# An encoder layer with expert retrieval on one core: row gathers without a pacing copy, value pieces fetched one at a time, the two halves of a weight made apart, and four accumulator banks filled ahead of the last group

## The chip, the cores and the metric

The kernel runs on one core of a Trainium2 chip. The metric is the device time of one execution in microseconds (us). Three timed runs of the kernel before gave 3643.04, 3645.47 and 3650.47 us; the median, 3645.47 us, is what the changed kernel is compared with. One further execution was recorded by the hardware profiler; all rows below come from it.

## The reference, cut to what matters

The layer has an attention half and a retrieval half (PEER). The change touches only the retrieval half, which takes 512 tokens of width 2048 and, per token, 8 heads with 16 experts each out of 16384:

```python
def block(args):
    xt, et, gt = args                                   # tokens, expert numbers, gates
    a = jnp.einsum('td,thkd->thk', xt, u_tab[et])
    w = gt * jax.nn.gelu(a, approximate=False)
    return jnp.einsum('thk,thkd->td', w, v_tab[et])
...
x = layer_norm(DN_ALPHA * x + g2 * p, ln2_g[l], ln2_b[l])
```

## The kernel before, in words

**Two ways to the same sum.** For the first 352 tokens (TD) the kernel computes every expert densely: u times tokens for all 16384 experts, gelu, times a gate that is zero where an expert was not chosen, times v. For the other 160 tokens it gathers only the chosen rows of u and v, one expert row per token and instruction: 320 gathers of 128 rows of 8 KB (1 MB each), 160 of u and then 160 of v. The dense part is the work of TensorE, the gathered part that of VectorE (DVE), which multiplies a gathered row by the token and sums (L1058), or adds a row, scaled, to an accumulator (L1064).

**Precision.** Each fp32 matmul is done as three in a reduced format: a tensor is split in a high part (a copy on ScalarE, ACT) and a low part (a subtraction on DVE), and hi*hi, hi*lo and lo*hi are summed. So each piece of weights needs a DMA (`raw`), a copy on ACT (`whi`, L99) and a subtraction on DVE (`wlo`, L100) before TensorE can use it.

**The stream.** The class Stream (L49) hands out pieces of 128x1024 (512 KB) in the order of a plan. `get` takes the next piece and then calls `fill`, which emits the split of the piece three places ahead (`split` is 3) and the loads up to six ahead (`ahead` is 6, L876). There are five buffers each for raw, high and low parts, so piece i takes over the buffers of piece i-5. Within the plan an expert row block of u has two pieces (`u`, x=0 and 1), and so has a tile of v.

**Groups and tiles.** 128 blocks of 128 experts make 32 groups of four (GE). Fourteen groups (0 to 13) have their u part computed in earlier stages and stored; the other 18 are in `gorder`. The main loop (L1230) goes over these 18: for each of four j it computes the u block (`u_mm`, 48 matmuls of 352 columns), the gelu (ACT, L1235), and then `v_mm` (L1166) for tile j of the group before. `v_mm` makes four units dd of 12 matmuls; a unit has its own PSUM bank, one of six, and needs all four weights W of a group (`W_0` to `W_3`, each high and low). Both v pieces are taken at its start (L1170): the first serves the W with x=0 and 1, the second those with x=2 and 3. After each unit ACT copies the bank to `accT` (L1185; L1187 in group 12) and fills the bank of the unit four later with the sum so far (`copy_in`, L1163). Between the units the functions of the list `beside` are emitted, one after each unit: the product of gelu and gate (`gl`, DVE, L1143), then `pair`, the high part (ACT, L1146) and the low part (DVE, L1147) of the next group's W. A short loop (L1246) does the last v group of the 18 with no u beside it, and the final part (L1370) goes over the stored groups 0 to 13, with v alone.

**The rows.** `step` (L1217) emits the gathers that are due at a fixed rate: twice per tile in the main loop (after the gelu and after `v_mm`), once per tile in the short loop and, at 0.85 of the rate, in the final part. `gather` (L1073) takes one of three row buffers, emits the pacing copy, the indirect DMA (both on GpSimd, POOL) and the use of the row of two calls before (LAG is 2) on DVE. The pacing copy (`paced`, L292 to L296) writes one column of the row buffer out of the newest `wlo`, so that the DMA cannot start before that split is done.

**What sets the order.** In these stages `inorder` is 2, and every instruction under `pin(op, 2)` keeps its place in the program on its engine. The rest (stores, loads of `x1`, the multiplication at L94, nearly all of the last group) is placed by the tile scheduler. On POOL, in order: the row copies and row DMAs, the loads of gates (`load_g`, L1134), the loads of stored gelu (`load_0` L1227, `load_gl` L1359), which wait until the low part W has been made out of the same buffer.

**The last group.** In group 13 the output is computed with tokens on the partitions: `start_sum` (L1342) fills a bank with `x1` (ACT, L1345), adds the transposed `accT` by matmuls (L1348, L1351), and `v_part` (L1204) adds group 13. Its v pieces are first multiplied by a gate (DVE, L94).

```python
        v = [st.get("v", g, j, x) for x in range(2)]
...
                vh, vl = v[x // 2]
                wh, wl = W[g, x]
                s = slice(x % 2 * 512 + dd * P, x % 2 * 512 + (dd + 1) * P)
```

Of the kernel before, what the change touches and what calls it, by code (L numbers as in the profile page):

```python
# [15 lines left out]
AF = mybir.ActivationFunctionType  # L16
# [3 lines left out]
P = 128  # L20
# [106 lines left out]
def tile_encoder_layer(ctx: ExitStack, tc: tile.TileContext, a: dict, out: bass.AP):  # L127
# [84 lines left out]
    def pin(op, level=1):  # L212


        if inorder[0] >= level:
            tc.keep_in_program_order(op)
        return op
# [74 lines left out]
    def paced(t, src=None, eng=nc.vector):  # L292


        src = st.parts[max(st.parts)][1] if src is None else src
        return eng.tensor_copy(t[:, 0:1], src.bitcast(F32)[:, 0:1])  # L296
# [775 lines left out]
    def gather(n=1):  # L1072

        for _ in range(n):
            i = ng[0]
            if i < NROW:
                ng[0] += 1
                row = gr.tile([P, D], F32, tag="row", name=f"row{i}")
                pin(paced(row, None, nc.gpsimd), 2)
                w, n_, c = gitems[i]  # L1080
                off = bass.IndirectOffsetOnAxis(ap=tiles[n_][0][:, c : c + 1], axis=0)
                src = a["peer_u"] if w == "u" else a["peer_v"]
                pin(nc.gpsimd.indirect_dma_start(out=row, out_offset=None, in_=src, in_offset=off), 2)
                rows_in.append((gitems[i], row))
            if len(rows_in) > (LAG if i < NROW else 0):
                gather_use()
# [39 lines left out]
    for q4 in range(XQ):  # L1126
        nc.gpsimd.dma_start(h2x[q4 * XT : (q4 + 1) * XT], h2x_d)
    ww = ctx.enter_context(pool("W", 2 * GE))
    W = {}

    def load_g(wk, g, gt=None):
        if gt is None:
# [4 lines left out]
    def weigh(gl, gt, g, j):  # L1137

        hi, lo = W[g, j] = [ww.tile([P, TD], F32R, tag="W" + n, name=f"W{g}_{j}{n}") for n in "hl"]

        def product():
            v3 = gl.rearrange("p (t c) -> p t c", t=NCH)
            pin(nc.vector.tensor_tensor(out=v3, in0=v3, in1=gt[:, :, j, :], op=ALU.mult), 2)  # L1143

        def pair():
            pin(nc.scalar.activation(hi, gl, AF.Copy), 2)  # L1146
            pin(nc.vector.tensor_tensor(out=lo, in0=gl, in1=hi.bitcast(F32), op=ALU.subtract), 2)  # L1147

        return [product, pair]

    banks("peer", q=2, o=6)
    ob_ = [bank("o") for _ in range(6)]
# [6 lines left out]

    def copy_in(u):  # L1160

        if 16 <= u < nunits:
            pin(nc.scalar.activation(ob_[u % 6][:, :TD], accT[:, u % 16], AF.Copy), 2)  # L1163

    def v_mm(g, j, by=None, beside=()):

        v = [st.get("v", g, j, x) for x in range(2)]
        beside = list(beside)  # L1170
        for dd in range(4):
            u = nu[0]
            o = o_bank()[:, :TD]
            sum_ = accT[:, j * 4 + dd]
            for x in range(GE):
                vh, vl = v[x // 2]
                wh, wl = W[g, x]
                s = slice(x % 2 * 512 + dd * P, x % 2 * 512 + (dd + 1) * P)
                first, last_ = u < 16 and x == 0, x == GE - 1
                kw = dict(skip_group_check=u >= 16)  # L1180
                pin(nc.tensor.matmul(o, vh[:, s], wh, start=first, stop=False, **kw), 2)  # L1181
                pin(nc.tensor.matmul(o, vh[:, s], wl, start=False, stop=False, **kw), 2)  # L1182
                pin(nc.tensor.matmul(o, vl[:, s], wh, start=False, stop=last_, **kw), 2)  # L1183
            if by is None:
                pin(nc.scalar.activation(sum_, o, AF.Copy), 2)  # L1185
            else:
                pin(nc.scalar.activation(sum_, o, AF.Copy, scale=by[:, j * 4 + dd : j * 4 + dd + 1]), 2)  # L1187
            copy_in(u + 4)
            f = beside.pop(0) if beside else None
            if f is not None:  # L1190
                f()
        for f in beside:
            f()
# [19 lines left out]
    def step(w=1.0):  # L1213
        pace[0] += rate * w
        gather(int(pace[0]))
        pace[0] -= int(pace[0])
# [4 lines left out]
    with pool("peer", 2, "right") as wk:  # L1221
        def gl_of(g, j):
            return wk.tile([P, TD], F32, tag="gl", name=f"gl{g}_{j}", bufs=2)

        def load_0(j):
            gls[0, j] = gl_of(0, j)
            pin(nc.gpsimd.dma_start(gls[0, j], ga_d[j]), 2)  # L1227

        gls = {}
        for n, g in enumerate(gorder):  # L1230
            gt = load_g(wk, g)
            for j in range(GE):
                gl = gl_of(g, j)
                ps = u_mm(g * GE + j)
                pin(nc.scalar.activation(gl, ps[:, :TD], AF.Gelu), 2)  # L1235
                if n > 0 or j > 1:
                    step()
                work = weigh(gl, gt, g, j)
                if n > 0:
                    v_mm(gorder[n - 1], j, None, work)  # L1240
                    step()
                else:
                    for f in work:
                        f()
        gt = load_g(wk, 0)
        load_0(0)  # L1246
        load_0(1)
        for j in range(GE):
            work = [None, None] + weigh(gls[0, j], gt, 0, j)
            if j < 2:  # L1250
                work.append(lambda j=j: load_0(j + 2))
            v_mm(gorder[-1], j, None, work)
            step()


    with pool("fin", 1, "right") as wk:
# [15 lines left out]
        def cols(j, n=1):  # L1272
            return slice(j * 512, (j + n) * 512)
# [17 lines left out]
            eng.dma_start(out[t * P : (t + 1) * P, c], r[:, c])  # L1291

        last = NF // GE - 1
        x1 = {}
        stts = [wk.tile([P, 4, 6], F32, name=f"stt{t}") for t in range(NT)]
        st.by = {("v", last, j, x): g2[:, cols(j)] for j in range(4) for x in range(2)}

# [44 lines left out]
        def start_sum(t, j):  # L1342

            o = o_bank()
            nc.scalar.activation(o, x1[t][:, cols(j)], AF.Copy)  # L1345
            kw = dict(start=False, stop=False, skip_group_check=True)
            if t == ND - 1:
                nc.tensor.matmul(o, sel, accx[:, cols(j)], **kw)  # L1348
            for dd in range(4):
                ts_ = slice(t * P, t * P + rows_of(t))  # L1350
                nc.tensor.matmul(o[: rows_of(t), dd * P : (dd + 1) * P], accT[:, j * 4 + dd, ts_], ident, **kw)  # L1351
            return o
# [3 lines left out]
        def load_gl(g, j):  # L1356
            if g <= last:
                gls[g, j] = wk.tile([P, TD], F32, tag="gl", name=f"gl{g}_{j}", bufs=GE)
                pin(nc.gpsimd.dma_start(gls[g, j], ga_d[g * GE + j]), 2)  # L1359
# [5 lines left out]
        for g in range(last + 1):  # L1365


            gt1, gt = gt, load_g(wk, g + 2, gts[g % 2]) if g + 2 <= last else None
            work = []
            for j in range(GE if g < last else 0):  # L1370
                product, pair = weigh(gls[g + 1, j], gt1, g + 1, j)
                work.append([lambda j=j, g=g: parts(g, j), None, product, pair, lambda j=j, g=g: load_gl(g + 2, j)])
            if g == 0:

                wh = W[g, 0][0]
                for o in ob_:
                    nc.tensor.matmul(
                        o[:, TD:], wh[:, :P], wh[:, : S - TD], start=False, stop=True, skip_group_check=True
                    )
            if g == 2:  # L1380
                for r, n in ((l2g, "ln2_g"), (l2b, "ln2_b")):
                    nc.gpsimd.dma_start(r, a[n].to_broadcast([P, D]))
            if g == last:
                inorder[0] = 0
            for j in range(GE):
                if g < last:
                    v_mm(g, j, mod[:, 80:96] if g == last - 1 else None, work[j])
                    if g < VN:
                        step(VW)
                elif j < 2:  # L1390
                    os_ = [start_sum(t, j) for t in range(ND)]
                    v = [st.get("v", g, j, x) for x in range(2)]
                    for x in range(GE):
                        for t in range(ND):
                            v_part(os_[t], g, x, t, v[x // 2])
                    for t, o in enumerate(os_):
                        nc.vector.bn_stats(stts[t][:, j, :], o)
                        nc.scalar.activation(x1[t][:, cols(j)], o, AF.Copy)
# [20 lines left out]
def _lay(inp):  # L1419
# [21 lines left out]
    def piece(n, *k):  # L1441
# [31 lines left out]
    rel = np.clip(np.arange(P)[:, None] - np.arange(S)[None, :] + 384, -63, 256) + 63  # L1473
    u = f("peer_u")[0]
    v = f("peer_v")[0]
    freq = (np.float32(10000.0) ** (-np.arange(0, 64, 2, dtype=np.float32) / np.float32(64.0))).astype(np.float32)
    rot = np.zeros((P, 2), np.float32)
    rot[:, 0] = np.tile(freq, 4)
# [16 lines left out]
        "ln1_g": f("ln1_g"), "ln1_b": f("ln1_b"), "ln2_g": f("ln2_g"), "ln2_b": f("ln2_b"),  # L1495
        "keys_t": f("peer_keys")[0].reshape(16, P, P).transpose(2, 0, 1).reshape(P, 16 * P),
        "u_t": u.reshape(P, P, 2, 8, P).transpose(1, 2, 4, 3, 0).reshape(P, 2, P, 1024),
        "v_t": v.reshape(P, NG, 2, 2, 4, 512).transpose(1, 4, 2, 0, 3, 5).reshape(NG, 4, 2, P, 1024),
        "peer_u": u,
        "peer_v": v,  # L1500
    }
# [17 lines left out]
```

## Time and profile before

| what | value |
|---|---|
| timed runs, median (lowest to highest) | 3645.47 us (3643.04 to 3650.47) |
| the profiled execution, its own time | 3657.82 us |
| its span, first to last instruction | 3656.0 us |
| TensorE matmul busy (share of the span) | 3568.4 us (98%) |
| VectorE, ScalarE, GpSimd busy | 2695.8, 1727.1 and 1002.2 us (74%, 47%, 27%) |
| pacing copies of rows (L296, POOL) | 320, 326.4 us, 1020 ns each |
| DMA, mean over the span | 273 GB/s |

The profiled execution is 12.35 us longer than the median run. Busy times are shares of a stretch; a stage is read by the windows that cut the span, and what an engine lacked by the waits, which name for each line what ended the idle time before it. Times in rows are us from the span's start. A matmul is shown some 0.32 us long while the next starts 0.16 us after it, so a short stop of TensorE can stay hidden in its busy time; the count of matmuls in a stretch tells more.

### The profile page before, as it was taken

How to read it: one execution, taken by the hardware profiler on the slowest of the kernel's cores; microseconds unless marked ns; L12 is line 12 of the kernel's file. 1: busy time of each engine (PE TensorE's matmuls, PEld its weight loads, DVE VectorE, ACT ScalarE, POOL GpSimd, SP SyncE). 2: the span in 40 equal slices, each digit the busy share in tenths (PEclk: the TensorE clock that was granted, in tenths of full speed). 3: DMA queues.
4: the chain of work that ended last, by engine and by line, in shares of the span. 5: the costliest groups of instructions: out<-in, count | busy, mean ns of one | idle time of the engine just before them, and what ended most of it. 6: DMA issues, size and time to landing. Idle time of an engine off the chain costs nothing. (4 is left out here: it accounts for less than half of the span.)

```text
span 3656.0 us, 52881 instructions
## 1 busy us (share of the span) xinstructions
PE 3568.4 (98%) x20127; PEld 3285.5 (90%) x20127; DVE 2695.8 (74%) x3754; ACT 1727.1 (47%) x3072; POOL 1002.2 (27%) x1068
## 2 busy tenths in 40 slices
PE   8999999999999999999999999999999999899998
PEld 6888888887787889999999999999999999899997
DVE  8756587545555779988888678888777788677776
ACT  3233332233333455435666345555544455566763
POOL 0001110011120000002322344444454544455531
PEclk9999999999999999999999999999999999999999
DMA  9646488744356655446998899999989999799982
GB/s 395 259 164 227 165 303 301 261 141 130 115 193 241 203 197 159 130 132 234 339 349 329 313 355 357 351 365 360 355 327 343 331 362 368 298 345 341 346 326 93
DMA packets 216207, 996.71 MB, mean 273 GB/s; under 512 B 26817, under 2 KB 34161, under 8 KB 159345
## 3 DMA queue, kind: packets, MB, share of 16 engines
q1 hardware_dynamic: 131904, 525.93, 40.4%
q0 software_dynamic: 73104, 431.48, 31.5%
q10 hardware_dynamic: 10944, 35.94, 2.5%
q8 instruction: 157, 2.57, 0.3%
q14 instruction: 98, 0.79, 0.1%
HBM read 930.42 MB, written 61.51 MB: 271 GB/s over the span
## 5 line engine op out<-in xcount | busy, mean ns | idle before, releaser
L99 ACT ACTIVATE whi<-raw 128x1024 fp32r<-128x1024 f32 x800 | 822.7, 1055 | 773.8 <-PE main L160 491.9
L100 DVE TENSOR_TENSOR wlo<-raw,whi 128x1024 fp32r<-128x1024 f32 x800 | 959.4, 1221 | 284.1 <-ACT whi L99 280.0
L159 PE MATMUL q<-dh,whi 128*128 128x352 f32 x1680 | 546.2, 325 | 0.6 <-ACT glf L926 0.6
L161 PE MATMUL q<-dh,wlo 128*128 128x352 f32 x1680 | 542.1, 323 | 0.7 <-DVE wlo L100 0.7
L160 PE MATMUL q<-dl,whi 128*128 128x352 f32 x1680 | 542.5, 323 | 0.0
L296 POOL COPY row<-wlo 128x1 f32<-128x1 f32 x320 | 326.4, 1020 | 714.5 <-DVE wlo L100 519.7
L1064 DVE SCALAR_TENSOR_TENSOR h2g<-row,au,h2g 128x2048 f32<-128x2048 f32 x127 | 298.4, 2349 | 101.9 <-DMA row<-in_peer_v,gidx 99.3
L159 PE MATMUL main<-hh,whi 128*128 128x512 f32 x912 | 352.9, 394 | 10.1 <-ACT hh L354 9.9
L160 PE MATMUL main<-hl,whi 128*128 128x512 f32 x912 | 357.1, 392 | 0.0
L161 PE MATMUL main<-hh,wlo 128*128 128x512 f32 x912 | 349.4, 393 | 0.0
L1058 DVE SCALAR_TENSOR_TENSOR row<-row,h2g 128x2048 f32<-128x2048 f32 x128 | 292.6, 2288 | 76.8 <-DMA row<-in_peer_u,gidx 76.4
L161 PEld LDWEIGHTS q<-dh,wlo 128*128 128x128 f32 x1680 | 316.6, 188 | 1.0 <-DVE wlo L100 1.0
L159 PEld LDWEIGHTS q<-dh,whi 128*128 128x128 f32 x1680 | 316.5, 188 | 1.0 <-ACT glf L926 0.8
L160 PEld LDWEIGHTS q<-dl,whi 128*128 128x128 f32 x1680 | 317.0, 189 | 0.0
L1185 ACT ACTIVATE accT<-o 128x352 f32<-128x352 f32 x480 | 219.5, 458 | 184.2 <-PE o L1183 178.6
L300 DVE SCALAR_TENSOR_TENSOR adaw<-adaw,cond 128x2048 f32<-128x2048 f32 x96 | 218.8, 2291 | 100.7 <-DMA adaw<-in_w_ada_t 96.9
L159 PE MATMUL main<-qh,whi 128*128 128x352 f32 (+2 forms) x752 | 242.9, 323 | 7.5 <-ACT qs L950 7.4
L161 PE MATMUL main<-qh,wlo 128*128 128x352 f32 (+2 forms) x752 | 242.7, 323 | 0.0
L160 PE MATMUL main<-ql,whi 128*128 128x352 f32 (+2 forms) x752 | 242.0, 322 | 0.0
L1163 ACT ACTIVATE o<-accT 128x352 f32<-128x352 f32 x480 | 223.0, 465 | 0.0
L159 PEld LDWEIGHTS main<-hh,whi 128*128 128x128 f32 x912 | 172.1, 189 | 47.3 <-ACT hh L354 11.5
L161 PEld LDWEIGHTS main<-hh,wlo 128*128 128x128 f32 x912 | 171.7, 188 | 35.8
(1359 smaller groups left out, 8045.9 us busy)
## 6 DMA issues: line engine op xcount, KB each, us to landing
raw<-in_wst SPq DMA_DIRECT2D x288, 512.0 KB
raw<-in_u_t SPq DMA_DIRECT2D x256, 512.0 KB
raw<-in_v_t SPq DMA_DIRECT2D x256, 512.0 KB
adaw<-in_w_ada_t SPq DMA_DIRECT2D x96, 1024.0 KB
g_d<-stg ACTq DMA_DIRECT2D x11, 2048.0 KB
gt<-g_d POOLq DMA_DIRECT2D x19, 704.0 KB
ga_d<-glf ACTq DMA_DIRECT2D x56, 176.0 KB
gl<-ga_d POOLq DMA_DIRECT2D x56, 176.0 KB
```

Of the source, the lines that this page charges most:

```text
L99: self.pin(self.nc.scalar.activation(hi, raw, AF.Copy), 2)
L100: self.pin(self.nc.vector.tensor_tensor(out=lo, in0=raw, in1=hi.bitcast(F32), op=ALU.subtract))
L159: pin(nc.tensor.matmul(ps, lh, rh, start=first, stop=False), 2)
L160: pin(nc.tensor.matmul(ps, lh, rl, start=False, stop=False), 2)
L161: pin(nc.tensor.matmul(ps, ll, rh, start=False, stop=last), 2)
L296: return eng.tensor_copy(t[:, 0:1], src.bitcast(F32)[:, 0:1])
L300: pin(nc.vector.scalar_tensor_tensor(w, w, 1.0, cond, op0=ALU.mult, op1=ALU.mult, accum_out=mod[:, j : j + 1]))
L1058: op = nc.vector.scalar_tensor_tensor(row, row, 1.0, h_, op0=ALU.mult, op1=ALU.mult, accum_out=a_[:, c : c + 1])
L1064: op = nc.vector.scalar_tensor_tensor(accs[n], row, a_[:, c : c + 1], accs[n], op0=ALU.mult, op1=ALU.add)
L1163: pin(nc.scalar.activation(ob_[u % 6][:, :TD], accT[:, u % 16], AF.Copy), 2)
L1185: pin(nc.scalar.activation(sum_, o, AF.Copy), 2)
```

## The change

Four edits. `gather` no longer emits the pacing copy where `inorder` is 2; the indirect DMA is then held by its buffer and its place on POOL alone. `v_mm` takes the two v pieces one at a time, at dd 0 and dd 2, and the host lays v out so that one piece holds two output blocks dd for all four W (group 13 keeps the old layout). `pair` becomes `high` and `low`, and their places move: in the main loop product, high, then the `step` that stood after `v_mm`, then low; in the short loop step, product, high, low; in the final part product, high, low one place earlier, without the empty place. And `copy_in` also fills the banks of the first four units of group 13 with `x1`, four units ahead, in program order; `start_sum` leaves these out.

```diff
-                pin(paced(row, None, nc.gpsimd), 2)
+                if inorder[0] < 2:
+                    paced(row, None, nc.gpsimd)
...
-        def pair():
+        def high():
             pin(nc.scalar.activation(hi, gl, AF.Copy), 2)
+
+        def low():
             pin(nc.vector.tensor_tensor(out=lo, in0=gl, in1=hi.bitcast(F32), op=ALU.subtract), 2)
 
-        return [product, pair]
+        return [product, high, low]
...
-        if 16 <= u < nunits:
+        if nunits <= u < nunits + 6:
+            t, j = (u - nunits) % ND, (u - nunits) // ND
+            pin(nc.scalar.activation(ob_[u % 6], x1[t][:, j * 512 : (j + 1) * 512], AF.Copy), 2)
+        elif 16 <= u < nunits:
...
-        v = [st.get("v", g, j, x) for x in range(2)]
...
+            if dd % 2 == 0:
+                vh, vl = st.get("v", g, j, dd // 2)
             for x in range(GE):
-                vh, vl = v[x // 2]
                 wh, wl = W[g, x]
-                s = slice(x % 2 * 512 + dd * P, x % 2 * 512 + (dd + 1) * P)
+                s = slice(x * 256 + dd % 2 * P, x * 256 + (dd % 2 + 1) * P)
...
-                    v_mm(gorder[n - 1], j, None, work)
-                    step()
+                    v_mm(gorder[n - 1], j, None, work[:2] + [step, work[2]])
...
-            work = [None, None] + weigh(gls[0, j], gt, 0, j)
+            work = [step] + weigh(gls[0, j], gt, 0, j)
...
             v_mm(gorder[-1], j, None, work)
-            step()
...
             o = o_bank()
-            nc.scalar.activation(o, x1[t][:, cols(j)], AF.Copy)
+            if nu[0] > nunits + 4:
+                nc.scalar.activation(o, x1[t][:, cols(j)], AF.Copy)
...
-                product, pair = weigh(gls[g + 1, j], gt1, g + 1, j)
-                work.append([lambda j=j, g=g: parts(g, j), None, product, pair, lambda j=j, g=g: load_gl(g + 2, j)])
+                work.append([lambda j=j, g=g: parts(g, j)] + weigh(gls[g + 1, j], gt1, g + 1, j)
+                            + [lambda j=j, g=g: load_gl(g + 2, j)])
...
+    vt = v.reshape(P, NG, GE, 4, 2, 256).transpose(1, 3, 4, 0, 2, 5).reshape(NG, 4, 2, P, 1024).copy()
+    last = NF // GE - 1
+    vt[last] = v.reshape(P, NG, 2, 2, 4, 512)[:, last].transpose(3, 1, 0, 2, 4).reshape(4, 2, P, 1024)
```

## Rows read from the trace of the kernel before

**Rows 1.** Windows by stage; columns stand in the first line, idle time is not shown.
```profile
core 0: us, PE busy (x) PEld busy (x) DVE busy (x) ACT busy (x) POOL busy (x), PEclk, DMA share, GB/s
2043.00:2440.00 397.00, 395.23 (x2474) 393.24 (x2474) 319.97 (x316) 196.81 (x346) 180.59 (x160) 1.00 0.93 349
2440.00:2617.00 177.00, 177.00 (x1115) 177.00 (x1114) 145.37 (x141) 90.18 (x162) 79.94 (x75) 1.00 0.95 362
2617.00:3000.00 383.00, 371.12 (x2299) 368.45 (x2298) 296.49 (x218) 188.24 (x337) 191.94 (x151) 0.99 0.91 338
3000.00:3120.00 120.00, 120.00 (x757) 120.00 (x757) 97.56 (x75) 61.69 (x112) 53.07 (x54) 1.00 0.97 368
3120.00:3178.00 58.00, 47.50 (x239) 43.23 (x239) 34.27 (x30) 26.30 (x54) 17.29 (x22) 0.88 0.78 295
3178.00:3588.00 410.00, 396.10 (x2410) 387.80 (x2408) 314.51 (x280) 274.13 (x549) 197.54 (x176) 0.99 0.89 327
3588.00:3656.00 68.00, 55.00 (x284) 45.11 (x284) 37.23 (x52) 23.69 (x40) 10.35 (x9) 0.91 0.18 70
```

**Rows 2.** Waits from 2043 to 3588: total us, times, longest us.
```profile
POOL row L296 <- DVE wlo L100: 426.2, 124, 16.2
DVE h2g L1064 <- DMA row<-in_peer_v,gidx: 99.3, 48, 7.6
PE o L1183 <- DVE wlo L100: 21.6, 19, 3.1
PE o L1181 <- ACT W_3h L1146: 7.7, 6, 1.7
PEld o L1182 <- DVE W_3l L1147: 4.8, 13, 0.4
```

**Rows 3.** DVE's timeline in the main loop: start, length, instruction, idle before.
```profile
2706.18 2.34 DVE L1064 SCALAR_TENSOR_TENSOR h2g<-row,au,h2g 128x2048 f32<-128x2048 f32 x1
2713.11 2.35 DVE L1064 SCALAR_TENSOR_TENSOR h2g<-row,au,h2g 128x2048 f32<-128x2048 f32 x1 [4.59 <-DMA row<-in_peer_v,gidx]
2715.38 2.36 DVE L100 TENSOR_TENSOR wlo<-raw,whi 128x1024 fp32r<-128x1024 f32 x2
...
2722.19 0.52 DVE L1143 TENSOR_TENSOR gl<-gl,gt 128x352 f32<-128x352 f32 x1
```

**Rows 4.** TensorE's timeline, the matmul that stopped in the same stretch.
```profile
2716.66 0.43 PE L1183 MATMUL o<-W_2h,wlo 128*128 128x352 f32 x1 [2.13 <-DVE wlo L100]
```

**Rows 5.** POOL's timeline, the same stretch.
```profile
2700.14 4.94 POOL L296 COPY row<-wlo 128x1 f32<-128x1 f32 x1 [5.59 <-DVE wlo L100]
2705.36 0.96 POOL L1083 DMA_INDIRECT row<-in_peer_v,gidx  x1 [0.27 <-POOL row L296]
```

**Rows 6.** The row DMA's line: durations in ns, min/median/max.
```profile
L1083 POOL DMA_INDIRECT row<-in_peer_v,gidx x128: 957/966/3102, 2607.7 to 3321.3; - x128
```

**Rows 7.** The chain that ended last, at a group's end in the final part.
```profile
3459.01 0.46 ACT o L1163
3459.47 0.42 ACT W_3h L1146
3459.92 0.54 DVE W_3l L1147
```

**Rows 8.** DVE's timeline where the short loop begins.
```profile
3125.46 2.35 DVE L1064 SCALAR_TENSOR_TENSOR h2g<-row,au,h2g 128x2048 f32<-128x2048 f32 x1 [7.59 <-DMA row<-in_peer_v,gidx]
...
3134.01 0.53 DVE L1143 TENSOR_TENSOR gl<-gl,gt 128x352 f32<-128x352 f32 x1 [3.92 <-DMA gl<-ga_d]
```

**Rows 9.** ACT's timeline ahead of the last group.
```profile
3587.86 0.55 ACT L1187 ACTIVATE accT<-o,mod 128x352 f32<-128x352 f32 x1 [8.18 <-DVE gl L1143]
...
3593.06 1.13 ACT L1345 ACTIVATE o<-x 128x512 f32<-128x512 f32 x2
```

**Rows 10.** TensorE's timeline there.
```profile
3588.83 0.66 PE L1181 MATMUL o<-W_0h,whi 128*128 128x352 f32 x1 [3.60 <-ACT o L1163]
...
3596.25 1.95 PE L1351 MATMUL o<-ident,accT 128*128 128x128 f32 x16
```

More of the change, by code (lines that the diff above doesn't have):

```diff
@@ L1128, in tile_encoder_layer @@
     ww = ctx.enter_context(pool("W", 2 * GE))
-    W = {}
+    W, x1 = {}, {}
     def load_g(wk, g, gt=None):
@@ L1293, in tile_encoder_layer @@
         last = NF // GE - 1
-        x1 = {}
         stts = [wk.tile([P, 4, 6], F32, name=f"stt{t}") for t in range(NT)]
@@ L1497, in _lay @@
         "u_t": u.reshape(P, P, 2, 8, P).transpose(1, 2, 4, 3, 0).reshape(P, 2, P, 1024),
-        "v_t": v.reshape(P, NG, 2, 2, 4, 512).transpose(1, 4, 2, 0, 3, 5).reshape(NG, 4, 2, P, 1024),
+        "v_t": vt,
         "peer_u": u,
```

## The prediction

> **What bounds the kernel now.** I read the windows by stage first [rows 1], then the waits [rows 2], then one stall up close [rows 3 to 5]. From 2043 us on, where the change acts, TensorE is the bound. In two stretches it never stops: 1115 matmuls in 177.00 us, or 0.1587 us each, and 757 in 120.00 us, which is the same [rows 1]. That is the yardstick: what a stretch takes beyond its matmuls times 0.1587 us is lost. 2043 to 2440: 397 - 2474 x 0.1587 = 4.3 us. 2617 to 3000: 383 - 364.9 = 18.1. 3120 to 3178: 58 - 37.9 = 20.1, of which some 3 belong to eight matmuls that make the gate row and are no loss. 3178 to 3588: 410 - 382.6 = 27.4. Together 70 us, 1.9% of the span; no edit here can give more. This count holds the stops themselves and their echo: in 3120 to 3178 the granted clock averages 0.88 [rows 1], so part of that time ran at 1.2 instead of 2.4 GHz, each time after TensorE had stood still.
>
> **Who stops TensorE.** Most of it is L1183, which waits for a `wlo`: 21.6 us in 19 stops, the longest 3.1; then L1181 and L1182 for the last weight of a group, `W_3h` 7.7 us in 6 and `W_3l` 4.8 us in 13 [rows 2]. The close view shows how the first kind comes about: DVE stands 4.59 us for a row's DMA, then makes two `wlo` in 2.36 us [rows 3], and TensorE has waited 2.13 us for the second, which the third weight, `W_2h`, needs [rows 4]. The row is late because it was asked for late: POOL sat 5.59 us until a `wlo` was done, then spent 4.94 us on a copy of one column, then issued at 2705.36; the use began 7.75 us after that [rows 3, 5]. So a late `wlo` delays a row, and a late row delays the next `wlo`.
>
> **Part 1, no pacing copy.** 50 of the 320 rows are asked for before 2043 us and keep it; 270 lose it. POOL's wait for `wlo` goes, 426.2 us in 124 waits [rows 2], 3.4 us each, and the copy of 4.94 us here [rows 5]. What holds a row DMA next is its buffer, free when the row three before has been used, and POOL's own queue (loads of gates and of stored gelu). With three rows per tile of 15.2 us (96 matmuls) in the main loop, a row gets 15.2 - 2.35 us (one use [rows 3]) = 12.9 us from its buffer's release to its use. The one shown took 7.75 us from issue to use, and DVE was ready for it 4.59 us earlier, so it had 3.2 [rows 3, 5]. That leaves 5.1 us to spare, and I take most of the row waits, 99.3 us on L1064 [rows 2], as gone. The pacing copies are off the critical path in themselves.
>
> First what the row shows: DMA_INDIRECT takes 957 ns at least and 3102 at most [rows 6], so an issue is at times held some 2.1 us, about one row use. The Trainium skill (SBUF — State Buffer, "SBUF: two separate sides") says that GpSimd and VectorE share one port pair under an exclusive lock, and that descriptors for DMAs from GpSimd cannot be written while VectorE holds it. That speaks against unpaced rows, which are issued just as DVE starts its next instruction: by it each would come up to 2.35 us later than I count, and nearly half of the spare 5.1 us would be gone. The median of 966 ns [rows 6] says that it is rare.
>
> **Part 2, one v piece at a time.** Same DMAs, copies and subtractions, other places. The split of a piece is emitted three `get`s ahead. Before, the second v piece was emitted at the first `get` of the tile before and its `wlo` needed by the eighth matmul of the next tile: 48 x 0.1587 + 8 x 0.1587 = 8.9 us. Now it is needed two pieces of 24 matmuls later plus two matmuls, counted from a `get` that comes at the same moment: 74 x 0.1587 = 11.7 us, and so for every piece. That is 2.8 us more for just the piece that was late by 3.1 at most and 1.14 on average (21.6/19) [rows 2]. What it gives away: the first v piece had 98 matmuls, 15.6 us, and now has 11.7 too. A new wait: the second piece's high part stands on ACT behind the copies of two units; behind it stand the next bank fills, which are four units (7.6 us) ahead. Cost nothing, with that cover; if it were gone, about one copy of 1 us per tile.
>
> **Part 3, high and low apart.** In the final part the chain at each group's end is bank fill 0.46, `W_3h` 0.42, `W_3l` 0.54 [rows 7], after the last unit, and TensorE meets it at the tenth matmul of the next. High now comes one unit (12 matmuls, 1.9 us) earlier and low needs only it. The 0.4 us stop at each of 13 group ends (4.8 us) and most of the 7.7 us for `W_3h` (longest 1.7 [rows 2], under 1.9) go. The loads behind the low part on POOL, and the rows behind them, come earlier too. In the main loop low now stands behind one or two row uses of 2.35 us and their waits; who waits for it is the next group, with the u block's 48 matmuls (7.6 us) between, so nothing. In the short loop the row use comes ahead of the product and there is no u block: there DVE stood 7.59 us for a row and 3.92 for a stored gelu [rows 8]. A row that late would now hold the product, then high on ACT, then the bank fills behind it. Bounds: from -6 (row asked for ahead of the stored-gelu load) to +8 us (one such wait passed on whole); I take a gain of 0 from this placement and leave the stretch what part 2 gives it.
>
> **Part 4, banks filled ahead.** ACT's fill of the first banks stood at 3593.06 before [rows 9], and TensorE went into the last group at 3596.25 with no stop [rows 10]: worth 0. The 3.60 us stop at 3588.83 [rows 10] is another: ACT had stood 8.18 us [rows 9] with a copy queued behind it. The two gated pieces now come apart there too; bounds 0 and 3.6 plus its clock echo, I take 2 of it.
>
> **The sum.** Main loop with u rows: 4.3 lost, 3 regained. With v rows to 3000: 18.1 lost, all of the one kind, 16 regained. Short loop: of 20.1 I take 8, since the gate row and the late DMAs stay. Final part: 27.4 lost; 4.8 and 7.7 for the weights, with `wlo` and echo about 5.5 more: 18. Together 45 us. The profiled execution had 3657.8 us around a span of 3656.0, so it would take 3612.8; it stands 12.35 above the median, and I take the same 45 us off the median: 3645.5 - 45 = 3600.5 us.
>
> **The rivals.** *The stop only moves* (no change). DVE has 296.49 us of work in the 2299/96 = 23.9 tiles from 2617 to 3000 [rows 1], 12.4 us in a tile of 15.2; with pieces coming one by one it must stand still in mid-tile for the second high part, and its slack of 2.8 us could then not serve late rows. TensorE would wait for another `wlo`: about 3645. Against it: the 11.7 us. *Half of it*: rows come no sooner, held on POOL by DVE or by the loads in its queue; only parts 2 and 3 in the final part and some of the stalls give: 20 us, about 3625. By the port rule above that is what would happen; the median of 966 ns is against it.
>
> *Slower: rows crowd out the pieces.* With all rows asked for early, three (3 MB) can be in flight, and `raw` pieces share the same engines. DMA is at 0.95 to 0.97 of its time at 362 and 368 GB/s [rows 1], so full is near 380; the final part at full pace needs per tile two pieces, 1.29 rows, and 0.35 MB of gates and gelu, 2.76 MB in 7.62 us = 362 GB/s. It decides once a piece lands later than five pieces (19 us) after its request. Then each tile loses something like the present mean stop of 1.14 us: in half of the 124 tiles 71 us, against 45 gained, 3671 us. Against it: the two stretches that ran without a stop did so at just this load. The Trainium skill (Perfetto Trace Analysis, "Roofline") puts the ceiling of one core's 16 DMA engines at about 435 GB/s; by it 362 would be 83% and this rival would hardly exist. The shares of this trace give less room, so I keep it.
>
> **How the numbers follow.** Forecast 3600 (roughly 3582 to 3618) 0.62, half 0.16, the stop only moves 0.10, slower 0.12. What a measurement of this kernel can tell from no change is about 0.2%, 7.3 us. Faster: 0.62 + 0.16 = 0.78; same 0.10; slower 0.12. The lower end is 3582, 63 of the 70 us; the upper end 3642 leaves out the slower case and part of the unchanged one.
>
> **What would show it.** Right: no L296 on POOL after 2043 us, waits of L1058 and L1064 for row DMAs cut to a third, L1183 for `wlo` under 5 us, no `W_3h` and `W_3l` stops at group ends, PEclk 0.95 or more in the short loop, the part after 3588 as long as before (68 us). Wrong: `whi` waiting for DMA raw (then the crowding), DMA_INDIRECT with a median near 3 us (the port), or TensorE's count per stretch unchanged while L1183's waits have gone to another line.

## The result, and the profile after

The changed kernel took 3613.68 us (median of 4 runs, 3608.2 to 3627.11), against 3647.97 us of the kernel before (4 runs, 3643.04 to 3654.65): a ratio of 0.990, 95% interval 0.9869 to 0.993. That is 34.3 us less, and by the interval 25 to 48 us. The prediction was 45 us less.

The profiled execution, at 3627.11 us the longest of the four, spans 3624.6 us, 31.4 less than before. Its windows answer to [rows 1]; the stages begin a little elsewhere, since some time had been lost before 2043 us (below).

```profile
core 0: us, PE busy (x) PEld busy (x) DVE busy (x) ACT busy (x) POOL busy (x), PEclk, DMA share, GB/s
2054.00:2440.00 386.00, 385.01 (x2420) 384.43 (x2419) 312.40 (x310) 195.95 (x339) 140.53 (x82) 1.00 0.92 353
...
2617.00:3000.00 383.00, 383.00 (x2412) 383.00 (x2411) 312.06 (x230) 199.02 (x354) 146.53 (x82) 1.00 0.93 360
...
3107.00:3166.00 59.00, 47.78 (x263) 44.87 (x262) 36.37 (x33) 30.77 (x60) 20.98 (x18) 0.91 0.85 311
3166.00:3557.00 391.00, 386.79 (x2393) 385.23 (x2393) 312.85 (x278) 279.46 (x548) 172.82 (x120) 0.99 0.92 341
3557.00:3624.60 67.60, 55.88 (x301) 45.95 (x299) 39.31 (x55) 24.81 (x41) 10.35 (x9) 0.93 0.21 78
```

The line to look at is that of 2617 to 3000 us: where 2299 matmuls went through before [rows 1], there are now 2412, and TensorE never stops. The final part runs 2393 matmuls in 391 us. The short loop, 3107 to 3166, is still bad: 47.78 of 59 us busy at a mean clock of 0.91. The tail is as it was.

The waits from 2054 to 3557 us (total us, times, longest) answer to [rows 2]:

```profile
POOL row L1084 <- DVE h2g L1064: 263.7, 60, 9.5
DVE h2gx L1064 <- DMA row<-in_peer_v,xidx: 30.3, 14, 5.7
DVE h2g L1064 <- DMA row<-in_peer_v,gidx: 13.1, 9, 4.4
PE o L1188 <- DVE W_3l L1150: 10.5, 4, 8.7
PE o L1187 <- ACT W_3h L1147: 2.4, 2, 2.2
```

GpSimd now waits for the use that frees a row buffer (L1064) and no longer for a `wlo`. The first row wait of [rows 2], 99.3 us, is 13.1; the waits for the last 32 rows (`h2gx`) rose from 10.0 to 30.3 us, and all row waits of L1058 and L1064 together fell from 183.6 to 45.8; TensorE's stops for a `wlo` in the v tiles, 21.6 us, are gone. In their place one stop of 8.7 us for `W_3l` has come.

For the rest a table by stage, of all kernels that ran, each from its one profiled execution. It is worked out from TensorE's timeline: the time from the first matmul of `v_mm` in one group to the first in a later one. `start` is the first of these matmuls, `u rows` the next nine groups, `v rows` seven more, `short` the group of the short loop and group 0 after it (with the matmuls that make the gate row), `final` groups 1 to 12, up to the last matmul of `v_mm`. `all` is the whole; it also holds the last group of the main loop, which stands in no column (53.41 us, but 63.54 in e2 and 57.66 in e3). A group that never stops takes 61.04 us in the main loop and 30.51 in the final part.

```
                          start  u rows  v rows   short   final      all
before                   2065.8  552.35  445.25   84.05  395.22  1530.29
after                    2077.4  549.35  427.28   82.06  375.60  1487.70
e1  rows alone           2062.8  549.35  427.28   83.66  385.64  1499.34
e2  v pieces alone       2065.5  619.55  496.79   94.57  394.56  1669.01
e3  all but rows         2068.1  597.64  477.39   89.98  403.15  1625.82
e4  all but v pieces     2069.8  549.35  427.28   83.84  373.80  1487.68
e5  e2, older wlo        2067.2  553.99  437.89   88.55  391.88  1525.73
e6  all but high/low     2065.1  549.52  427.28   83.63  381.55  1495.40
e7  after, low first     2064.6  549.36  427.28   78.15  375.48  1483.68
e8  after, loads later   2066.5  549.36  427.28   68.85  383.24  1482.14
e9  copy of a constant   2066.5  549.35  427.28   87.48  397.21  1514.73
e10 all but banks        2066.0  549.36  427.28   80.96  371.36  1482.37
e11 e7 + loads last      2069.7  549.52  427.28   67.91  375.35  1473.47
e12 e11, both pieces     2068.5  549.35  427.28   79.17  374.33  1483.55
```

From the first `v_mm` on the changed kernel's profiled execution is 42.6 us shorter. The span shows only 31.4 of it, because this execution came to its first `v_mm` 11.6 us later. No edit reaches back that far, and the other kernels begin at 2062.8 to 2069.8 us; so that is a difference between executions.

### The profile page after: what moved, and what is told of

Its sections match the earlier page's. It is cut to its first block, busy times and chain, and to the rows that moved or that the text cites. A ratio compares the mean times of both kernels' runs of the same rounds, so it can differ in the third digit from the quotient of the medians.

```text
span 3624.6 us, 52483 instructions
## 1 busy us (share of the span) xinstructions
PE 3550.7 (98%) x20127; PEld 3277.3 (90%) x20127; DVE 2689.7 (74%) x3754; ACT 1740.0 (48%) x3072; POOL 863.4 (24%) x798
## 4 chain that ended last, share of the span: by engine, by line
PE 79%; DMA 8%; issue 6%; DVE 4%; POOL 2%; ACT 0%; POOLq 0%; SPq 0%; DVEq 0%; ACTq 0%
PE main L161 11%; PE main L159 11%; PE main L160 11%; PE o L1187 7%; PE o L1188 7%; PE o L1189 7%; PE q L159 6%; PE q L161 6%; PE q L160 6%; DMA adaw<-in_w_ada_t 4%; DMA row<-in_peer_v,xidx 2%; DVE adaw L300 1%; DVE wlo L100 1%; PE g L1107 1%; POOL row L1084 1%
## 5 line engine op out<-in xcount | busy, mean ns | idle before, releaser
L100 DVE TENSOR_TENSOR wlo<-raw,whi 128x1024 fp32r<-128x1024 f32 x800 | 969.3, 1220 | 474.7 <-ACT whi L99 468.6
L99 ACT ACTIVATE whi<-raw 128x1024 fp32r<-128x1024 f32 x800 | 835.6, 1055 | 773.5 <-PE main L160 477.2
L161 PE MATMUL q<-dh,wlo 128*128 128x352 f32 x1680 | 541.4, 322 | 0.7 <-DVE wlo L100 0.7
L161 PE MATMUL main<-hh,wlo 128*128 128x512 f32 x912 | 349.5, 393 | 3.1 <-DVE wlo L100 3.1
L161 PEld LDWEIGHTS q<-dh,wlo 128*128 128x128 f32 x1680 | 316.1, 188 | 1.0 <-DVE wlo L100 1.0
L1084 POOL DMA_INDIRECT row<-in_peer_v,gidx x128 | 240.1, 1876 | 307.4 <-DVE h2g L1064 263.7
L1064 DVE SCALAR_TENSOR_TENSOR h2g<-row,au,h2g 128x2048 f32<-128x2048 f32 x127 | 298.2, 2348 | 14.5 <-DMA row<-in_peer_v,gidx 13.1
L1058 DVE SCALAR_TENSOR_TENSOR row<-row,h2g 128x2048 f32<-128x2048 f32 x128 | 290.8, 2286 | 22.5 <-DMA row<-in_peer_u,gidx 22.5
L1084 POOL DMA_INDIRECT row<-in_peer_u,gidx x128 | 203.9, 1593 | 272.5 <-DVE row L1058 244.1
L161 PE MATMUL main<-qh,wlo 128*128 128x352 f32 (+2 forms) x752 | 242.8, 323 | 0.0
```

The source lines that it names most:

```text
L99: self.pin(self.nc.scalar.activation(hi, raw, AF.Copy), 2)
L100: self.pin(self.nc.vector.tensor_tensor(out=lo, in0=raw, in1=hi.bitcast(F32), op=ALU.subtract))
L161: pin(nc.tensor.matmul(ps, ll, rh, start=False, stop=last), 2)
L1058: op = nc.vector.scalar_tensor_tensor(row, row, 1.0, h_, op0=ALU.mult, op1=ALU.mult, accum_out=a_[:, c : c + 1])
L1064: op = nc.vector.scalar_tensor_tensor(accs[n], row, a_[:, c : c + 1], accs[n], op0=ALU.mult, op1=ALU.add)
```

## The experiments

The first four take the parts alone and away. The kernels were timed on four occasions, each time with the kernel before beside them, and the kernel before differs by up to 21 us between these (medians 3647.97, 3655.4, 3669.0 and 3653.6 us); so a ratio holds for its own occasion, and kernels of different occasions are compared by stage.

**Rows alone.** The kernel before, with the first edit only:

```diff
-                pin(paced(row, None, nc.gpsimd), 2)
+                if inorder[0] < 2:
+                    paced(row, None, nc.gpsimd)
```

> The kernel before with one edit: no pacing copy and no pacing wait for rows. Theory A (either a row in time or 2.8 us more lead for the second v piece is enough): the stops for wlo in the main loop go, 16 to 20 us, and the stops for W_3h and W_3l at the group ends of the final part stay (12 us): about 3625 us, ratio 0.993 to 0.995. Theory B (the two edits only work together): little, ratio 0.998 to 1.00, with L1183 still waiting 15 us or more for wlo. Rival port (a row DMA without the copy meets VectorE's next instruction and is held): DMA_INDIRECT's median near 3 us and the row waits on L1064 unchanged near 99 us.

Measured: ratio 0.9931 (0.9915 to 0.9948). The main loop is at its floor in all 16 groups, in the windows of this kernel too:

```profile
2617.00:3000.00 383.00, 383.00 (x2412) 383.00 (x2411) 316.22 (x229) 197.68 (x353) 141.66 (x82) 1.00 0.93 359
```

So this edit alone gives all that the change gives in the main loop, 21 us, and 9.6 us in the final part. Theory B falls, for this side.

**v pieces alone.** The kernel before, with the second edit only:

```diff
-        v = [st.get("v", g, j, x) for x in range(2)]
...
+            if dd % 2 == 0:
+                vh, vl = st.get("v", g, j, dd // 2)
...
-                s = slice(x % 2 * 512 + dd * P, x % 2 * 512 + (dd + 1) * P)
+                s = slice(x * 256 + dd % 2 * P, x * 256 + (dd % 2 + 1) * P)
```

> The kernel before with one edit: v pieces fetched one at a time (with the new layout of v), rows still paced, weights as before. Theory A: 2.8 us more lead covers stops of 1.1 us on average, so the main loop's 18 us from 2617 to 3000 us and the final part's 3 us for wlo go: ratio 0.993 to 0.995, row waits unchanged near 200 us in all. Theory B (VectorE now stands in mid-tile for the second high part, 2.8 us of slack per tile gone, and with 2.4 us of row waits per tile it falls behind): slower in the main loop, some 1 to 2 us in each of 33 tiles with v rows, ratio 1.01 or more.

Measured: ratio 1.0403 (1.0385 to 1.042). The part that I had counted as 2.8 us of lead for TensorE makes the kernel 4% slower, with u rows as with v rows. Its waits from 2070 us on:

```profile
POOL row L296 <- DVE wlo L100: 560.8, 93, 13.5
DVE h2g L1064 <- DMA row<-in_peer_v,gidx: 126.4, 44, 8.7
PE q L161 <- DVE wlo L100: 46.7, 32, 6.5
PE o L1189 <- DVE wlo L100: 41.6, 40, 2.7
```

GpSimd waits 560.8 us for a `wlo` instead of 426.2 [rows 2], VectorE more for rows, and TensorE stops for `wlo` in u blocks (L161) and v tiles (L1189) alike. It is theory B by size, but that says nothing yet of its reason.

**All but rows, all but v pieces.** The changed kernel with one edit taken back each.

> The changed kernel with the pacing copy and its wait put back: v pieces one at a time, weights apart, banks ahead. Theory A: nearly all of the gain stays, about 3620 us, 0.99 to 0.994 of before. Theory B: the gain in the main loop is lost or turns into a loss, and rows late by 2 us stop the low parts behind them: 1.00 or more.

Measured: 1.027 (1.0252 to 1.0287). With rows paced, the rest of the change is a loss of 2.7%.

> The changed kernel with both v pieces taken at the start of a tile again (old layout), rows without pacing, weights apart, banks ahead. Theory A: nearly all of the gain stays, 0.99 to 0.994. Theory B: half of it, 0.995 to 0.998; L1183 for wlo would be back with 10 us or more.

Measured: 0.9885 (0.9868 to 0.9901). Without single v pieces the kernel is as fast as with them: 1487.68 against 1487.70 us from the first `v_mm` on. This run fits theory A, the run with v pieces alone does not: rows in time are enough, and the pieces' lead is not. One thing single pieces do give. Ahead of the last group, TensorE's stop of 3.60 us [rows 10] is gone in the changed kernel, and here 2.06 us of it are back:

```profile
3551.76 0.43 PE L1187 MATMUL o<-W_0h,whi 128*128 128x352 f32 x1 [2.06 <-ACT o L1169]
```

Group 12 takes 37.2 us before, 30.8 in the changed kernel and 34.5 here; groups 1 to 11 are 5.5 us shorter here, which evens it out.

**Why single pieces cost 4% with paced rows.** The pacing copy reads the newest `wlo`. With both pieces taken at a tile's start, that one is made early in the tile; with one at a time it is made in mid-tile. The next kernel keeps single pieces and the copy, and lets it read the second newest:

```diff
-                pin(paced(row, None, nc.gpsimd), 2)
+                older = st.parts[sorted(st.parts)[-2]][1] if inorder[0] == 2 else None
+                pin(paced(row, older, nc.gpsimd), 2)
```

> As the run with v pieces one at a time alone, still with a pacing copy for each row, but the copy reads the second newest wlo instead of the newest, so a row asked for after a tile waits for a split that was done half a tile earlier. Theory F (the loss comes through the pacing: the newest wlo is now made in mid-tile, rows are asked for later, VectorE stands for them, the next wlo is later still): most of the 139 us in the 124 tiles go, under 1.01 of before, and VectorE's row waits fall from 250 to under 150 us. Rival S (VectorE has lost its slack to the stop in mid-tile, whatever paces the rows): still 1.03 to 1.04. That the fetching of single pieces is harmless once rows are in time would fit theory F alone.

Measured: 0.9966 (0.9947 to 0.9986). Of the 139 us that single pieces cost, all are gone (1669.0 to 1525.7, before 1530.3). VectorE's row waits are 129.8 us in all, under the 150 of theory F. Three of its waits:

```profile
POOL row L296 <- DVE wlo L100: 291.3, 108, 9.6
DVE h2g L1064 <- DMA row<-in_peer_v,gidx: 69.2, 40, 8.9
PE o L1190 <- DVE wlo L100: 13.8, 12, 3.6
```

Theory F holds: the loss comes through the pacing. This copy waits less than that of the kernel before (291.3 us instead of 426.2), so the run alone shows only that looser pacing takes the loss away; that single pieces cost nothing without pacing is shown by the changed kernel beside that with all but v pieces. The loop itself is read from the waits: a later `wlo` lets a row be asked for later, VectorE stands for it, and the `wlo` behind it is later again, which paces the next row.

**The wait or the copy.** Rows keep their copy, but of a constant:

```diff
-                pin(paced(row, None, nc.gpsimd), 2)
+                pin(paced(row, None if inorder[0] < 2 else ident, nc.gpsimd), 2)
```

> The kernel before with one edit: each row keeps its copy on GpSimd, but in the stages with v it reads a constant tile instead of the newest wlo, so it waits for nothing but its buffer. Theory W (the wait for wlo is what made rows late): as with the copy left out, the main loop's groups at 61.04 us, ratio 0.993 to 0.995 of before. Rival C (the copy itself, held by VectorE's instruction, up to 4.9 us): wlo stops of 10 us or more stay in the main loop, ratio 0.997 to 1.00.

Measured: 0.9974 (0.9964 to 0.9984). That is the ratio of rival C and not of theory W, but the main loop is at its floor, as theory W said:

```profile
2617.00:3000.00 383.00, 383.00 (x2411) 383.00 (x2410) 316.92 (x228) 198.38 (x353) 171.54 (x159) 1.00 0.93 360
```

So there it was the wait and not the copy that made rows late. The short loop and the final part are 15.4 us longer than without the copy (87.48 + 397.21 against 83.66 + 385.64). There the queue of GpSimd also holds the loads of stored gelu. Single stops of 1 to 4 us and their echo at the lower clock make most of it, in one profile each, and how much of that is the copy stays open.

**High and low together again.** The changed kernel with `pair` and the steps at their old places.

> The changed kernel with the weights' high and low parts together again and the steps at their old places: rows without pacing, v pieces one at a time, banks ahead. By what the first runs showed, the main loop needs only the unpaced rows: its groups at 61.04 us as in the changed kernel. If the order of high and low clears the group ends of the final part, its 0.4 us stops come back there, 12 groups by 0.8 to 1 us, some 8 to 10 us slower than the changed kernel in that part (375.6 us there). In the short loop the 8.7 us stop for W_3l goes, if it is the row use ahead of the low part that made it.

Measured: 0.9887 (0.9852 to 0.9922). The final part takes 381.55 us against 375.60, so the order of high and low gives about 6 us there, less than the 8 to 10 expected, and the stops of 0.4 us are back:

```profile
PE o L1191 <- ACT W_3h L1147: 5.4, 6, 1.7
PEld o L1192 <- DVE W_3l L1150: 5.2, 14, 0.4
```

The stop of 8.7 us in the short loop is gone, but the stretch is no shorter (83.63): ACT's bank fills stopped TensorE instead (9.4 us in 3).

**The new stop.** In the changed kernel's short loop GpSimd, VectorE and TensorE, each from its timeline:

```profile
3100.10 0.59 POOL L1386 DMA_DIRECT2D rb<-in_ln_g  x1 [11.36 <-PE q L161]
```

```profile
3115.30 2.35 DVE L1064 SCALAR_TENSOR_TENSOR h2g<-row,au,h2g 128x2048 f32<-128x2048 f32 x1 [4.17 <-DMA row<-in_peer_v,gidx]
3117.57 0.52 DVE L1150 TENSOR_TENSOR W_3l<-gl,W_3h 128x352 fp32r<-128x352 f32 x1
```

```profile
3118.14 0.66 PE L1188 MATMUL o<-W_3l,whi 128*128 128x352 f32 x1 [8.73 <-DVE W_3l L1150]
```

The load of the last layer norm's gain (L1386) stands in GpSimd's queue and waits 11.36 us for the last u block, whose buffers it takes. Rows behind it come late, VectorE waits 4.17 us for the first of them, and the low part of the main loop's last tile, which now stands behind that row's use, comes with it. GpSimd's wait itself is not new. The kernel before has it as well, and the row that VectorE waits 7.59 us for there [rows 8] is the first one issued behind the load:

```profile
3109.49 0.58 POOL L1382 DMA_DIRECT2D rb<-in_ln_g  x1 [8.15 <-PE q L161]
```

Two kernels tell the queue and the low part's place apart. One puts the low part first in that tile alone:

```diff
-                    v_mm(gorder[n - 1], j, None, work[:2] + [step, work[2]])
+                    v_mm(gorder[n - 1], j, None, work + [step] if (n, j) == (len(gorder) - 1, GE - 1) else work[:2] + [step, work[2]])
```

> The changed kernel, but in the last tile of the main loop alone the low part stands ahead of the row use again. Theory L (the 8.7 us stop for W_3l at the start of the short loop comes from the low part standing behind a late row, with no u block to cover it): the stop goes, and with its echo at the half clock the two groups around the short loop take 10 to 13 us less than the 82.1 us of the changed kernel. Rival: another wait comes last there (a stored gelu, a wlo), and less than 4 us are gained.

Measured: 0.9841 (0.9805 to 0.9877); the short loop takes 78.15 us, 3.9 less. The 8.7 us stop is gone, and others came in its place, as the rival said: 5.1 us for bank fills and 2.2 for `W_3l`. The other keeps the loads and the selection matrix at their places in the program:

```diff
-                    nc.gpsimd.dma_start(r, a[n].to_broadcast([P, D]))
+                    pin(nc.gpsimd.dma_start(r, a[n].to_broadcast([P, D])), 2)
...
-        nc.gpsimd.memset(sel, 0.0)
+        pin(nc.gpsimd.memset(sel, 0.0), 2)
```

> The changed kernel, with the loads of the last layer norm's gain and bias and the making of the small selection matrix kept at their places in the program on GpSimd and VectorE, where the scheduler had moved them up into the last tiles of the main loop. There GpSimd stood 11.4 us with these loads ahead of rows. Theory L2 (the late row in the short loop comes from this): GpSimd's stop goes, the row is there, the 8.7 us stop for W_3l goes: 8 to 13 us less in the short loop, as when the low part is moved. Rival: the row is late for another reason and the stop stays above 5 us.

Measured: 0.9842 (0.9806 to 0.9877); the short loop takes 68.85 us, 13.2 less, at full clock:

```profile
3107.00:3166.00 59.00, 57.15 (x345) 54.79 (x344) 45.73 (x48) 40.95 (x84) 23.90 (x20) 1.00 0.87 320
```

So GpSimd's queue was the cause and the low part's place only the way. (The edit moves the loads and the selection matrix together; which of them gives how much was not measured.) The loads themselves, now in group 3, made a stop there (41.09 us for that group instead of 30.72, with 7.1 us for `W_3h` in one wait).

**Banks.** The changed kernel without the fills ahead.

> The changed kernel without the filling of the last group's first four banks ahead. By the prediction this part is worth 0: group 12 and what follows (30.8 and 59.6 us in the changed kernel) the same within 1 us. Rival: with the pieces coming one by one the scheduler no longer finds a place for these copies early, and TensorE stops 1 to 3 us at the start of the last group.

Measured: 0.9879 (0.9851 to 0.9907). Group 12 takes 30.77 us with and without, and what follows 59.55 with and without. It is worth nothing.

**A version from this.** e7's edit, the selection matrix as in e8, and the loads behind the last row:

```diff
                 use_rows(NROW)
+                for r, n in ((l2g, "ln2_g"), (l2b, "ln2_b")):
+                    pin(nc.gpsimd.dma_start(r, a[n].to_broadcast([P, D])), 2)
                 load_x1(ND, 0, 1)
```

> The changed kernel with the low part first in the main loop's last tile, the selection matrix made in program order, and the loads of the last layer norm's gain and bias put behind the last row. If the stop in the short loop and the stop that these loads made in the third group of the final part are both due to GpSimd's queue, the short loop takes 69 us and the final part 373 to 376 us, 14 to 17 us less than the changed kernel, ratio 0.978 to 0.984. Rival: the 2 MB of these loads or the rows make another stop, and under 8 us are gained.

Measured: 3607.16 us, 0.9872 (0.985 to 0.9894). The short loop takes 67.91 us as expected; from the first `v_mm` on it is 1473.47 us, 14.2 less than the changed kernel. The ratio is not the one expected, and against the changed kernel's 3613.68 us, measured on another occasion, the timed runs don't tell the two apart.

> The kernel of the run before it with both v pieces taken at the start of a tile again. If fetching single pieces is worth nothing once rows are not paced, the same within 4 us. Theory A's last stand: the 2.8 us more lead helps in the final part, and this one is 5 us or more slower there.

Measured: 3611.5 us, 0.9876 (0.9851 to 0.990), 1483.55 us from the first `v_mm` on; the final part is 1.0 us shorter without single pieces, so theory A's last stand falls. But it is not the same within 4 us in the profile: the short loop takes 11 us more (79.17), where TensorE stopped 6.3 us for copies on ACT. The medians are 4.3 us apart and the runs overlap, so whether single pieces help there stays open.

## Why the prediction was right, and which step of it was wrong

The sign and the size held: 34.3 us of the 45, with an interval of 25 to 48 us, inside the range. By stage, from the first `v_mm` on, the profile gave 42.6: with u rows 3.0 (I said 3), with v rows 18.0 (16), around the short loop 2.0 (8), in the final part 19.6 (18); the tail, which is not in the 42.6, gave 0.4 (0). That close a match is luck in part, and hides a wrong reason: parts 1 and 2 were counted together for the main loop, and part 1 earned all of it.

**Part 1 was right, and worth more than I gave it.** Row waits fell to a quarter (a third was forecast), and the rows in time cleared the main loop alone (e1). The step on [rows 3 to 5], that a late `wlo` delays a row and a late row the next `wlo`, is the mechanism of the whole main loop.

**Part 2 is the step that failed.** I counted 11.7 instead of 8.9 us of lead and took single pieces as a second cover for the same stops; by what was expected of them alone (e2), they were worth the main loop's loss by themselves. Alone they cost 139 us (e2), and with rows unpaced they give nothing in the main loop and nothing over all (e4). I had listed the queues that the `get` is moved past, ACT and VectorE, and not asked who else waits for that `wlo`: the pacing copy. Moving the split to mid-tile moved the request of each row with it. The rival *The stop only moves* named VectorE's lost slack; e5 shows that the pacing carried it, since with the older `wlo` the same split in mid-tile costs nothing. (The 11.7 us are three pieces of 24 matmuls and two matmuls; the text said two pieces.)

**Part 3 was half right.** The stops at the group ends go, but for five of 0.2 to 2.2 us; the order of high and low gives 6 us in the final part (e6), where I put the 12.5 us of `W_3h` and `W_3l`, while unpaced rows give 9.6 there (e1). That low behind a row use costs nothing, with the u block as its cover, is true for 16 of the 17 groups with a low part so placed and false for the last, which has no u block behind it: there it made the 8.7 us stop. The term for the short loop, 8 us, came out at 2.0, and the clock there at 0.91 instead of the 0.95 named as a sign. What made the row late there, a load ahead of it in GpSimd's queue, none of the four edits touched; moving it gives 13.2 us (e8).

**Part 4** was worth nothing, as said (e10). Of the 3.60 us stop ahead of the last group I took 2, which the sum does not name; all of it went, and group 12 is 6.4 us shorter. It takes the single pieces as well as the new order: with both pieces taken at the start it is 34.5 us (e4), with high and low together 33.0 (e6), with both edits 30.8.

**The slower rival did not come.** With rows unpaced, DMA was busy 0.93 of the time at 360 GB/s from 2617 to 3000 us with no stop of TensorE. The risk that was there I had not listed: one edit that is a heavy loss without the other.

**The port.** Unpaced row DMAs are held more often: the median issue went from 966 [rows 6] to 1681 ns:

```profile
L1084 POOL DMA_INDIRECT row<-in_peer_v,gidx x128: 939/1681/3522, 2614.1 to 3300.5; - x128
```

The timelines show what they are held by. Of these 128 issues 123 began while VectorE was in an instruction, and 120 of them ended 0.80 to 0.88 us after that instruction did. Before, 79 of the 128 began with VectorE at rest (median 962 ns), and the copies ahead of them had taken such waits instead: 83 of 129 began while VectorE was in an instruction. So the median of 966 ns, which I held against the rule, was that of rows sheltered by a copy and said nothing of unpaced ones. The Trainium skill (SBUF — State Buffer, "SBUF: two separate sides") has a rule of this kind: where an instruction of VectorE with two inputs in SBUF meets one of GpSimd that reads SBUF, the one that starts first has the shared ports for its whole length, and the other blocks. The trace agrees in that all 78 issues of over 1.5 us began under an instruction of VectorE; that the ports are the reason is not shown. At the median it cost 0.7 us of a spare time of 5.1, so it decided nothing in the main loop.

## What to carry to other kernels

When an instruction is moved, list everything that waits on its result, and look first for instructions that exist only to pace others: a pace point tied to "the newest" of something moves whenever the making of it moves. Two edits that each look like a cover for the same stop should be asked what each does without the other; here one gives 31 us, the other costs 139 alone and is worth nothing over all beside it. And a cover such as "the next block hides it" must be checked at the last pass of its loop, where the scheduler also puts what waits for the loop's buffers.

## What the runs showed that I had not expected

Pacing can turn a delay that had cover into a cost: a split half a v tile (3.8 us) later, with 11.7 us of lead left, made the 16 groups with u and v rows 118.7 us longer, 7.4 us each (e2: 619.55 + 496.79 against 552.35 + 445.25 us). Loads placed early by the scheduler, waiting 11.36 us in GpSimd's queue, cost the short loop and group 0 13.2 us (e8), more than any other single thing that the runs took out of the changed kernel; the kernel before has the same wait (8.15 us), and its trace could have shown it. And the stretch before the first `v_mm`, which no edit touches, differed by up to 14.6 us between profiled executions (2062.8 to 2077.4), as much as some of the effects here; comparing by stage is what kept it out.
